# Conditioning rows and sums pinned, and the first stage of a two-layer backbone in a written-out order

## The chip, the cores and the metric

The kernel runs on one core of one Trainium2 chip. The metric is the device time of one execution in microseconds. Beside the plain runs one execution was taken by the hardware profiler; every row quoted here is from it. Engines are named as in the profile: PE is TensorE, DVE is VectorE, ACT is ScalarE, POOL is GpSimd, SP is the engine that issues most transfers. PEclk is the granted clock of TensorE as a share of full speed; it has two levels, 1.2 and 2.4 GHz.

## What is computed

A bidirectional hybrid backbone of two layers over 128 context tokens and 512 latent tokens, 1024 wide. What matters here, from the reference:

```
mod = silu(cond) @ ada_w + ada_b              # cond: c_ctx for context tokens, c for latent tokens
sh_m, sc_m, g_m, sh_f, sc_f, g_f = mod in six parts of 1024
h = rmsnorm(x, norm_mix) * (1 + sc_m) + sh_m
x = x + g_m * (token_mixers(h) @ w_out)       # mixers: one projection h @ w_in, HGRN2 and retention heads
h = rmsnorm(x, norm_ffn) * (1 + sc_f) + sh_f
x = x + g_f * ((silu(gate) * up) @ w_down)    # gate, up = h @ w_up
```

Outputs are the tokens after a final norm and the final states of the context tokens.

## The kernel before, in words

The 640 tokens are five tiles of 128 (tile 0 holds the context tokens). All weights come from memory as float32 through one stream (`Stream`, lines 56 to 100): `load` issues a transfer of 512 KB on SP, `cut` splits it into a rounded part on ACT (line 75) and the rest on DVE (line 76), and each GEMM is three matmuls per block (high by high, high by low, low by high). `W_BUFS` is 4, `RAW_BUFS` 3.

The modulation is computed in three ways. The four blocks that layer 0's first norm needs (block 0 and 2: scale, columns 0 to 511 and 512 to 1023; block 1 and 3: shift) are matmuls in `ada_first` (lines 322 to 491): each block is loaded in four quarters; blocks 0, 1 and 3 (`FAST`) are cut like weights (`cut`, lines 344 and 345) and multiplied (`mm`, line 355), block 2 is multiplied uncut in single precision (line 358); the row is copied out (line 363), turned into columns by eight small matmuls (`rt`, line 369) and finished on DVE (`fin`). The scales and shifts of the later norms are column sums on DVE (`ada_cols`, line 536): a tile of the transposed weights times a row of silu(c), which stands in all partitions (`srow`, loaded and activated in `ada_rows`, lines 514 and 515); 32 sums for layer 0's second norm and 64 for layer 1's two. The gates are accumulated on DVE (`ada_chunk`, line 505).

The first stage runs under `manual_schedule`: what `ada_first` and the first GEMM trace keeps its order on every engine. It does, per token tile t: `sq(t)` squares and sums on ACT, POOL's power makes the norm's factor, `xs(t)` scales on DVE, `tr(t)` transposes on PE, `xc(t)` copies to SBUF on ACT; then, per half of the 1024 columns, `full(t, hf)` applies scale and shift (`kd` of four 128-blocks on DVE, the others on ACT), and `split(t, hf)` cuts the result into the GEMM's operand `hT`. The GEMM (`ws`, line 610) has three units u (zf, zb and qa of head 0), each in two token parts hf (tokens 0 to 255 and 256 to 639) and two halves of K, so twelve pieces. In before the pieces of the first half of K are issued as soon as the blocks 0 and 1 are done, with the matmuls of blocks 2 and 3 between them:

```
out = [(0, 0, 0, 4), lambda: mm(2, 2, 4), (1, 0, 0, 4), lambda: rt(2), lambda: fin(2), ...
```

Everything else is put in order by a scheduler, which may issue an instruction early on its engine, the manual stage included, when its inputs and its buffer are there. The program order comes from a planner (`Net.run`, line 138): each piece of GEMM yields a cost in planner units, and side tasks in lanes advance a step whenever their quantum has been reached (`Q_ADA` 3.0 units in the mixer, 2.0 in the output projection, 4.0 in the feed-forward part; the lane starts 25 units late, `ACC0`). A unit of three 128-column GEMMs and so on costs what its `yield` says: 5.1e-3 per token and K half in `ws`, 1.31 per four blocks in `as_`. In the mixer `ORDER` (line 38) sets the order of heads; its units after the first three GEMM units add up to 216. `pin` (line 303) keeps an instruction behind the one traced before it on its engine.

Of the kernel before, what the change touches and what calls it, by code (L numbers as in the profile page):

```python
# [46 lines left out]
Q_SCAN = 2.65  # L47
Q_ADA = (3.0, 2.0, 4.0)
ADP_BUFS = 2


def view(t, off, dims):
# [3 lines left out]
class Stream:  # L56
# [5 lines left out]
    def load(self):  # L62
        src, kk, nn = self.slots[self.loaded]
        raw = self.net.rawp.tile([P, 1024], F32, tag="raw", name="raw")
        self.net.nc.sync.dma_start(out=raw[:, :kk * nn].rearrange("p (k n) -> p k n", k=kk), in_=src)
        self.raw[self.loaded] = (raw, kk, nn)
        self.loaded += 1

# [34 lines left out]
class Net:  # L103
# [218 lines left out]
    def ada_first(self):  # L322
        nc, a = self.nc, self.a
        V = nc.vector
        raws, xn, rs, xt = [], {}, {}, {}

        def load(i):
            col = (1 - i % 2) * 1024 + (i // 2) * 512
            for j in range(4):
                w = self.B("adw")  # L330
                nc.sync.dma_start(out=w[:, :1024].rearrange("p (k n) -> p k n", k=2),
                                  in_=a["ada_w"][0, 2 * j * P:(2 * j + 2) * P, col:col + 512].rearrange(
                                      "(k p) n -> p k n", p=P))
                raws.append(w)
        pr, pc, row, cuts = {}, {}, {}, {}

        def cut(i, j):
            w = raws[4 * i + j]
            if i < 2 or j == 2:
                hi, lo = self.whp.tile([P, 1024], F32R, tag="wh", name="ahi"), \  # L340
                    self.wlp.tile([P, 1024], F32R, tag="wl", name="alo")
            else:
                hi, lo = self.ON("ahi", F32R)[:, :1024], self.ON("alo", F32R)[:, :1024]
            nc.scalar.copy(hi, w[:, :1024])
            V.tensor_tensor(lo, w[:, :1024], hi.bitcast(F32), op=ALU.subtract)
            cuts[i, j] = hi, lo

        def mm(i, j0, j1):
            if j0 == 0:
                pr[i] = self.ps("pr")  # L350
            for k in range(2 * j0, 2 * j1):
                sl = slice(k % 2 * 512, k % 2 * 512 + 512)
                if i in FAST:
                    for n, wv in enumerate(cuts[i, k // 2]):
                        nc.tensor.matmul(pr[i][:, :512], self.srv[:, k], wv[:, sl],
                                         start=k == 0 and n == 0, stop=k == KT - 1 and n == 1)
                else:
                    nc.tensor.matmul(pr[i][:2, :512], self.sT[:, :, k], raws[4 * i + k // 2][:, sl],
                                     start=k == 0, stop=k == KT - 1)
            if j1 == 4:  # L360
# [29 lines left out]
        def tr(t):  # L390
            xt[t] = self.norm_b(t, xn[t])
# [22 lines left out]
            nc.scalar.copy(hi, f)  # L414
            V.tensor_tensor(lo, f, hi.bitcast(F32), op=ALU.subtract)

        load(0)
        for t in range(NT):
            self.load_x(t)
        load(1)  # L420
        for _ in range(3):
            self.W.load()
        load(2)
        self.new_hT()
        for j in range(4):
            cut(0, j)
            if j == 3:
                sq(0)
            mm(0, j, j + 1)
        xs(0)  # L430
        sq(1)
        tr(0)
        xs(1)
        sq(2)
        xc(0)
        tr(1)
        xs(2)
        sq(3)
        xc(1)
        tr(2)  # L440
        xs(3)
        sq(4)
        xc(2)
        tr(3)
        self.setup_cols()
        rt(0)
        fin(0)
        cut(1, 0)
        mm(1, 0, 1)
        xs(4)  # L450
        xc(3)
        cut(1, 1)
        tr(4)
        mm(1, 1, 2)
        cut(1, 2)
        xc(4)
        cut(1, 3)
        mm(1, 2, 3)
        self.W.cut()
        mm(1, 3, 4)  # L460
        self.W.cut()
        load(3)
        nc.sync.dma_start(out=self.mask, in_=a["mask"].rearrange("p (b s) -> p b s", b=5))
        nc.sync.dma_start(out=self.rope, in_=a["rope"].rearrange("p (b s) -> p b s", b=2))
        rt(1)
        fin(1)
        mm(2, 0, 2)
        full(0, 0)
        full(1, 0, 4)
        split(0, 0)  # L470
        split(1, 0)
        for t in range(2, NT):
            full(t, 0)
            if t > 2:
                split(t - 1, 0)
        self.W.cut()
        split(4, 0)
        lb = self.setup_lb()
        cut(3, 0)
        cut(3, 1)  # L480
        out = [(0, 0, 0, 4), lambda: mm(2, 2, 4), (1, 0, 0, 4), lambda: rt(2), lambda: fin(2),
               lambda: cut(3, 2), (0, 1, 0, 4), lambda: mm(3, 0, 2), lambda: cut(3, 3), lb, (1, 1, 0, 4),
               lambda: mm(3, 2, 4), lambda: rt(3), lambda: fin(3), (2, 0, 0, 4), (2, 1, 0, 4)]
        for t in range(NT):
            out.append(lambda t=t: full(t, 1, 4 if t == 1 else KD))
            if t:
                out.append(lambda t=t: split(t - 1, 1))
        out.append(lambda: split(NT - 1, 1))
        out += [(u, hf, 4, 8) for hf in range(2) for u in range(3)]
        out.append(self.W.pump)  # L490
        return out

    def ada_chunk(self, l, col, alloc, sink):
# [15 lines left out]
    def ada_rows(self):  # L509
        a = self.a  # L510
        self.srow = self.const.tile([P, 2, DM], F32, name="srow")
        self.junk = self.const.tile([P, DM], F32, name="junk")
        for c, src in enumerate((a["c_ctx"], a["c"])):
            self.nc.sync.dma_start(out=self.srow[:, c], in_=bass.AP(src.tensor, src.offset, [[0, P], [1, DM]]))
        self.nc.scalar.activation(self.srow, self.srow, AF.Silu)

    def ada_cols(self, l, m, alloc):
        V = self.nc.vector
        if self.srow is None:
            self.ada_rows()  # L520
# [89 lines left out]
    def ws(self, *evacs, mid=None, order=None):  # L610
# [4 lines left out]
        mm = self.nc.tensor.matmul  # L615
        base = self.W.used

        def part(u, hf, k0, k1):
            hi, lo = slots[u]
            sl = slice(cut, TOK) if hf else slice(0, cut)  # L620
            o = pss[u][:, 512 - cut + sl.start:512 - cut + sl.stop]
            for k in range(k0, k1):
                h_hi, h_lo = self.hT[:, 0, k, sl], self.hT[:, 1, k, sl]
                mm(o, hi[:, k], h_hi, start=k == 0, stop=False)  # L624
                mm(o, hi[:, k], h_lo, start=False, stop=False)  # L625
                mm(o, lo[:, k], h_hi, start=False, stop=k == KT - 1)  # L626
        def both(u, k0, k1):
            hi, lo = slots[u]
            sls = [slice(0, cut), slice(cut, TOK)]
# [18 lines left out]
        for i, op in enumerate(order):  # L648
            if callable(op):
                op()  # L650
                continue
            u, hf, k0, k1 = op
            while mid and hf and self.pend:
                self.flush1()
            if pss[u] is None:
                pss[u] = self.ps("gw")
                slots[u] = self.W.get(base + u)
            part(u, hf, k0, k1)
            if mid and i == 1:
# [622 lines left out]
```

## Time and profile before

| | |
|---|---|
| plain runs, median of 3 | 1849.0 us (1847.05 to 1849.16) |
| the profiled execution | 1847.48 us |
| its span, first to last instruction | 1845.7 us |
| mean granted clock of PE | 0.991 |
| PE busy | 1793.7 us (97%) |
| DVE busy | 1041.3 us (56%) |
| ACT busy | 712.1 us (39%) |
| POOL busy | 49.1 us (3%) |
| moved by transfers | 184.06 MB, mean 100 GB/s |

The page's slices show PE busy at 90% or more in all of the 40 but the first (0.5) and the last (0.8). The busy time of a pipelined matmul overlaps that of the next, and its end is modelled, so a full PE is not PE at its peak: the interval from one matmul's start to the next is what counts. An idle time in brackets in a timeline is the engine's time without work ahead of that instruction, with what ended it. A timeline merges neighbours of one line ("x8"); their time runs from the first start to the last end.

### The profile page before, as it was taken

The numbers are of one execution on the slowest core, as the hardware profiler recorded it, in microseconds if no ns is written. First come the engines' busy times: TensorE is split into PE (matmuls) and PEld (weight loads), VectorE is DVE, ScalarE is ACT, GpSimd is POOL, SyncE is SP. The second block draws the span as 40 slices with busy tenths as digits, with TensorE's granted clock in tenths as the row PEclk, the third lists the DMA queues.
The fourth block names the chain that finished last, engine by engine and source line by source line (L and its number), as shares of the span: only waits on it lengthen the run. The fifth ranks groups of instructions, "written<-read, shape, count | busy, mean of one in ns | idle before, by whom it ended". The sixth has DMA issues, their size and how long they took to land.

```text
span 1845.7 us, 29294 instructions
## 1 busy us (share of the span) xinstructions
PE 1793.7 (97%) x12301; PEld 1719.7 (93%) x12301; DVE 1041.3 (56%) x1614; ACT 712.1 (39%) x1208; POOL 49.1 (3%) x59
## 2 busy tenths in 40 slices
PE   5999999999999999999999999999999999999998
PEld 3799999998999978999899999999899998899988
DVE  3889757864854986222366656587475522323234
ACT  5675645633522211222246555455352221122221
POOL 1000000000000000000000000000000000000000
PEclk7999999999999999999999999999999999999999
DMA  8424223222433654222222121322234322222221
GB/s 288 155 81 152 78 78 112 92 69 69 137 115 117 224 182 140 80 70 75 75 81 72 50 69 53 109 78 89 80 92 126 115 75 75 80 80 69 75 75 58
DMA packets 204612, 184.06 MB, mean 100 GB/s; under 512 B 6736, under 2 KB 172336, under 8 KB 204480
## 3 DMA queue, kind: packets, MB, share of 16 engines
q1 hardware_dynamic: 199584, 179.67, 30.8%
q10 hardware_dynamic: 4640, 2.43, 0.4%
q8 instruction: 96, 1.57, 0.4%
q0 software_dynamic: 256, 0.09, 0.1%
q14 instruction: 36, 0.29, 0.1%
HBM read 177.44 MB, written 4.72 MB: 99 GB/s over the span
## 4 chain that ended last, share of the span: by engine, by line
PE 78%; DVE 10%; DMA 4%; ACT 4%; issue 3%; SPq 1%; POOL 1%; DVEq 0%; POOLq 0%; ACTq 0%
PE gw L634 36%; PE ga L680 5%; PE ga L679 5%; PE ga L678 5%; PE ga L1053 5%; PE ga L1055 4%; PE ga L1054 4%; PE pl L771 3%; DMA adt<-in_ada_t 2%; DVE junk L536 2%; DVE wl L76 2%; PE gw L625 1%; PE gw L624 1%; PE gw L626 1%; PE ga L1032 1%
## 5 line engine op out<-in xcount | busy, mean ns | idle before, releaser
L634 PE MATMUL gw<-hT,wh 128*128 128x320 f32 x3712 | 702.0, 311 | 0.0
L634 PEld LDWEIGHTS gw<-hT,wh 128*128 128x128 f32 x3712 | 581.3, 188 | 1.1
L75 ACT CAST wh<-raw 128x1024 fp32r<-128x1024 f32 (+2 forms) x224 | 231.7, 1035 | 704.4 <-PE gw L634 267.1
L76 DVE TENSOR_TENSOR wl<-raw,wh 128x1024 fp32r<-128x1024 f32 (+2 forms) x224 | 269.4, 1204 | 357.3 <-ACT wh L75 357.1
L634 PE MATMUL gw<-hT,wl 128*128 128x320 f32 x1856 | 423.8, 309 | 0.0
L634 PEld LDWEIGHTS gw<-hT,wl 128*128 128x128 f32 x1856 | 310.4, 188 | 0.1
L678 PE MATMUL ga<-wh,hT 128*128 128x256 f32 x640 | 185.7, 290 | 0.0
L680 PE MATMUL ga<-wh,hT 128*128 128x256 f32 x640 | 181.4, 284 | 0.0
L679 PE MATMUL ga<-wl,hT 128*128 128x256 f32 x640 | 181.4, 283 | 0.0
L1053 PE MATMUL ga<-wh,act 128*128 128x512 f32 x330 | 130.2, 395 | 4.1 <-DVE xa L996 4.1
L1054 PE MATMUL ga<-wl,act 128*128 128x512 f32 x330 | 129.6, 393 | 0.0
L1055 PE MATMUL ga<-wh,act 128*128 128x512 f32 x330 | 128.8, 393 | 0.0
L536 DVE CUSTOM_DVE_ANT_0 junk<-adt,srow 128x1024 f32<-128x1024 f32 x96 | 117.8, 1227 | 18.5 <-DMA adt<-in_ada_t 17.0
L1104 DVE TENSOR_TENSOR sgf<-sgf,gw 128x640 f32<-128x640 f32 x44 | 36.1, 820 | 162.3 <-PE gw L634 162.3
L678 PEld LDWEIGHTS ga<-wh,hT 128*128 128x128 f32 x640 | 122.7, 192 | 0.3
L679 PEld LDWEIGHTS ga<-wl,hT 128*128 128x128 f32 x640 | 122.6, 192 | 0.3
L680 PEld LDWEIGHTS ga<-wh,hT 128*128 128x128 f32 x640 | 122.4, 191 | 0.0
L505 DVE SCALAR_TENSOR_TENSOR acc<-adw,sTt,acc 128x512 f32<-128x512 f32 x112 | 79.6, 747 | 23.0 <-DMA adw<-in_ada_w 22.7
L1053 PEld LDWEIGHTS ga<-wh,act 128*128 128x128 f32 x330 | 62.6, 190 | 18.6 <-DVE xa L996 6.0
L1055 PEld LDWEIGHTS ga<-wh,act 128*128 128x128 f32 x330 | 62.7, 190 | 13.3
L771 PE MATMUL pl<-X 128*128 128x128 f32 x560 | 72.3, 276 | 2.4 <-ACT X L758 2.3
L1054 PEld LDWEIGHTS ga<-wl,act 128*128 128x128 f32 x330 | 62.6, 190 | 12.5
(226 smaller groups left out, 2639.0 us busy)
## 6 DMA issues: line engine op xcount, KB each, us to landing
raw<-in_w_up SPq DMA_DIRECT2D x88, 512.0 KB, 3.8
raw<-in_w_in SPq DMA_DIRECT2D x72, 512.0 KB, 3.7
adt<-in_ada_t SPq DMA_DIRECT2D x48, 512.0 KB, 4.0
raw<-in_w_down SPq DMA_DIRECT2D x38, 512.0 KB, 3.7
adw<-in_ada_w SPq DMA_DIRECT2D x64, 256.0 KB, 2.9
adw<-in_ada_w SPq DMA_DIRECT2D x16, 512.0 KB, 7.0
raw<-in_w_out SPq DMA_DIRECT2D x16, 512.0 KB, 3.5
gate<-in_ada_b SPq DMA_DIRECT2D x8, 512.0 KB, 5.2
```

The source lines that it names most:

```text
L75: nc.scalar.copy(hi[:, :n], raw[:, :n])
L76: nc.vector.tensor_tensor(lo[:, :n], raw[:, :n], hi[:, :n].bitcast(F32), op=ALU.subtract)
L505: nc.vector.scalar_tensor_tensor(d, w, s, d, op0=ALU.mult, op1=ALU.add)
L536: V.tensor_tensor_reduce(out=self.junk, in0=w[:, :DM], in1=self.srow[:, c], scale=1.0, scalar=0.0, op0=ALU.mult, op1=ALU.add, accum_out=se ...
L634: mm(o, w[:, k], self.hT[:, d, k, sl], start=k == 0 and i == 0, stop=k == KT - 1 and i == 2)
L678: mm(o, a_hi, hi[:, j], start=i == 0, stop=False)
L679: mm(o, a_hi, lo[:, j], start=False, stop=False)
L680: mm(o, a_lo, hi[:, j], start=False, stop=i == nk - 1)
L771: nc.tensor.matmul(pl[:, i * P:(i + 1) * P], X[:, TOK + i * P:TOK + (i + 1) * P], X[:, i * P:(i + 1) * P], start=True, stop=True)
L1053: mm(o, a_hi, hi[:, j], start=i == 0, stop=False)
L1054: mm(o, a_hi, lo[:, j], start=False, stop=False)
L1055: mm(o, a_lo, hi[:, j], start=False, stop=i == nk - 1)
```

## The change

- `srow`'s two transfers are issued behind the stream's last weight load so far, and the Silu comes four steps of the lane later and is pinned. Of the two column sums of each tile the first is pinned.
- The first stage is given by two lists: `BOOT_LOADS`, the order of the transfers (`Lij` is quarter j of block i, `xt` a token tile, `W` a weight), and `BOOT`, the order of the steps. `feed` issues loads as far as a limit on quarters held allows. All quarters' cuts use the weight buffers.
- The GEMM's pieces (`g` u hf K-half) all stand behind the last block's matmuls, in the order 010 110 210 001 101 200 100 201 011 000 111 211; a unit is evacuated when its four pieces are done, in whatever order (`seen`).
- The lower bounds (`setup_lb`) go ahead of `split31` and of `g011`; the mask and rotary tables are loaded behind all of `BOOT_LOADS`.

```diff
+BOOT_LOADS = (
+    "L00 x4 L01 L10 L02 L11 L12 L13 L03 L20 x2 x3 x0 x1 L21 L30 L22 L31 L32 L33 L23 W W W "
+).split()
+BOOT = (
+    "cut00 sq4 xs4 tr4 cut01 mm00 cut10 cols xc4 cut02 cut11 mm01 cut12 mm10 cut13 mm02 mm11 mm12 cut03 "
+    "mm13 sq2 xs2 mm03 sq3 mm20 rt1 xs3 tr2 fin1 sq0 sq1 rt0 xs0 tr3 fin0 mm21 xc2 full20-4 xs1 tr0 xc3 "
+    "cut30 full30-0 full40-4 cut31 tr1 cut32 cut33 mm30 split40 split30 mm22 mm31 xc0 W mm32 mm33 mm23 "
+    "rt3 fin3 rt2 split20 fin2 W g010 g110 xc1 full01-3 W g210 full11-4 full00-0 split01 split11 g001 "
+    "full21-4 full10-0 split10 split00 full31-4 split21 g101 g200 full41-0 g100 g201 split31 split41 g011 "
+    "g000 g111 g211 "
+).split()
...
         def cut(i, j):
-            w = raws[4 * i + j]
-            if i < 2 or j == 2:
-                hi, lo = self.whp.tile([P, 1024], F32R, tag="wh", name="ahi"), \
-                    self.wlp.tile([P, 1024], F32R, tag="wl", name="alo")
-            else:
-                hi, lo = self.ON("ahi", F32R)[:, :1024], self.ON("alo", F32R)[:, :1024]
+            w = raws.pop((i, j))
+            hi, lo = self.whp.tile([P, 1024], F32R, tag="wh", name="ahi"), \
+                self.wlp.tile([P, 1024], F32R, tag="wl", name="alo")
...
+        def feed(last=False):
+            while loads and (last or loads[0][0] != "L" or len(raws) < B_BUFS - 1 - min(NT, len(xt) + 2)):
+                o = loads.pop(0)
+                if o[0] == "L":
+                    load(int(o[1]), int(o[2]))
+                elif o[0] == "x":
+                    self.load_x(int(o[1]))
+                else:
+                    self.W.load()
...
+        out = []
+        for o in BOOT:
+            if o[0] == "g":
+                out.append((int(o[1]), int(o[2]), 4 * int(o[3]), 4 * int(o[3]) + 4))
+            elif out:
+                out.append(lambda o=o: step(o))
+            else:
+                step(o)
+        feed(True)
         nc.sync.dma_start(out=self.mask, in_=a["mask"].rearrange("p (b s) -> p b s", b=5))
         nc.sync.dma_start(out=self.rope, in_=a["rope"].rearrange("p (b s) -> p b s", b=2))
...
         out.append(self.W.pump)
+        lbs = []
+        out.insert(-7, lambda: lbs.append(self.setup_lb()))
+        out.insert(-5, lambda: lbs[0]())
         return out
...
         for c, src in enumerate((a["c_ctx"], a["c"])):
-            self.nc.sync.dma_start(out=self.srow[:, c], in_=bass.AP(src.tensor, src.offset, [[0, P], [1, DM]]))
-        self.nc.scalar.activation(self.srow, self.srow, AF.Silu)
+            with self.tc.issue_after(self.W.last.ins):
+                self.nc.sync.dma_start(out=self.srow[:, c], in_=bass.AP(src.tensor, src.offset, [[0, P], [1, DM]]))
...
         if self.srow is None:
             self.ada_rows()
-            yield
+            for _ in range(4):
+                yield
+            self.pin(self.nc.scalar.activation(self.srow, self.srow, AF.Silu))
...
             for c in range(2):
-                V.tensor_tensor_reduce(out=self.junk, in0=w[:, :DM], in1=self.srow[:, c], scale=1.0, scalar=0.0,
-                                       op0=ALU.mult, op1=ALU.add,
-                                       accum_out=self.modc[:, l, m, 1 - which, c, j:j + 1])
+                r = V.tensor_tensor_reduce(out=self.junk, in0=w[:, :DM], in1=self.srow[:, c], scale=1.0, scalar=0.0,
+                                           op0=ALU.mult, op1=ALU.add,
+                                           accum_out=self.modc[:, l, m, 1 - which, c, j:j + 1])
+                if c == 0:
+                    self.pin(r)
...
-            if hf == 1 and k1 == KT:
+            if seen.get((u, 0)) == KT and seen.get((u, 1)) == KT:
                 self.W.done()
                 evacs[u](pss[u][:, 512 - cut:512 - cut + TOK].rearrange("p (a b) -> p a b", a=2))
```

## Rows read from the trace of the kernel before

**Rows 1.** Table by stretches: length, PE, PEld, DVE, ACT, POOL, PEclk, DMA share, GB/s.

```profile
0.00:51.70 51.70, 29.49 (x99) 19.18 (x99) 22.25 (x43) 29.54 (x43) 8.26 (x20) 0.77 0.77 260
51.70:85.40 33.70, 31.63 (x185) 26.82 (x185) 27.38 (x60) 18.21 (x29) 4.03 (x2) 1.00 0.53 182
85.40:1845.70 1760.30, 1732.62 (x12019) 1673.67 (x12018) 991.70 (x1513) 664.33 (x1139) 36.84 (x37) 1.00 0.30 93
```

**Rows 2.** Timeline, first stage, ScalarE: start us, us, engine, line, operation [idle before].

```profile
5.58 1.04 ACT L344 CAST ahi<-adw 128x1024 fp32r<-128x1024 f32 x1 [2.61 <-DMA adw<-in_ada_w]
...
36.97 1.91 ACT L515 ACTIVATE srow<-srow 128x2048 f32<-128x2048 f32 x1 [10.47 <-DMA srow<-in_c]
```

**Rows 3.** Timeline, SP's queue, first stage.

```profile
26.91 0.74 SPq L514 DMA_DIRECT2D srow<-in_c_ctx  x1
```

**Rows 4.** Table by stretches, layer 0 feed-forward part, 670 to 700 us.

```profile
670.00:680.00 10.00, 5.90 (x26) 4.58 (x26) 8.45 (x18) 1.06 (x1) 0.00 (x0) 0.92 0.56 184
680.00:690.00 10.00, 10.00 (x34) 8.02 (x35) 7.52 (x13) 1.61 (x2) 0.00 (x0) 0.74 0.34 105
690.00:700.00 10.00, 10.00 (x46) 8.29 (x45) 8.58 (x14) 1.56 (x2) 0.00 (x0) 1.00 0.75 223
```

**Rows 5.** Waits from 580 to 730 us: total us, times, longest us.

```profile
DVE junk L536 <- DMA adt<-in_ada_t: 15.9, 12, 4.6
...
PE ga L1053 <- DVE xa L996: 4.1, 1, 4.1
```

**Rows 6.** Table by stretches, layer 0's mixer.

```profile
85.40:420.00 334.60, 326.73 (x2570) 323.64 (x2570) 253.68 (x434) 189.57 (x346) 14.88 (x9) 1.00 0.30 94
...
100.00:200.00 100.00, 96.67 (x739) 95.72 (x738) 84.80 (x170) 67.36 (x119) 6.60 (x3) 1.00 0.34 109
```

**Rows 7.** Table by stretches of line 536 alone (first column DVE).

```profile
100.00:200.00 100.00, 22.44 (x36) 1.00 0.34 109
```

**Rows 8.** Groups of instructions, 5 to 52 us: busy us, mean ns | idle.

```profile
L345 DVE TENSOR_TENSOR alo<-adw,ahi 128x1024 fp32r<-128x1024 f32 x8 | 9.7, 1223 | 15.5 <-ACT ahi L344 15.4
...
L344 ACT CAST ahi<-adw 128x1024 fp32r<-128x1024 f32 x8 | 8.3, 1052 | 4.0 <-DMA adw<-in_ada_w 4.0
...
L363 ACT COPY row<-pr 4x512 f32<-4x512 f32 x2 | 1.1, 566 | 2.1 <-PE pr L355 2.1
```

**Rows 9.** Timeline, TensorE, first stage: small matmuls and transposes.

```profile
21.71 1.06 PE L586 MATMUL pt<-ident,xn 128*128 128x128 f32 x8 [1.23 <-DVE xn L388]
...
26.71 1.91 PE L586 MATMUL pt<-ident,xn 128*128 128x128 f32 x8
...
46.14 5.64 PE L358 MATMUL pr<-adw,sTt 128*2 128x512 f32 x8
...
53.34 3.59 PE L358 MATMUL pr<-adw,sTt 128*2 128x512 f32 x8
...
58.49 1.05 PE L369 MATMUL pc<-sel,row 2*128 2x2 f32 x8
...
65.65 0.39 PE L355 MATMUL pr<-ahi,sr 128*128 128x512 f32 x1
...
67.26 0.40 PE L355 MATMUL pr<-alo,sr 128*128 128x512 f32 x1
```

**Rows 10.** Table by stretches, two stretches of the first stage.

```profile
16.00:20.00 4.00, 4.00 (x22) 3.95 (x23) 1.64 (x4) 2.99 (x6) 1.10 (x2) 0.57 1.04 392
...
33.00:40.00 7.00, 0.00 (x0) 0.00 (x0) 0.00 (x0) 3.03 (x3) 0.00 (x0) 0.52 0.75 290
```

**Rows 11.** Timeline, TensorE, GEMM of the first stage.

```profile
74.87 0.39 PE L625 MATMUL gw<-hT,wh 128*128 128x256 f32 x1 [1.28 <-DVE hT L415]
75.10 0.28 PE L626 MATMUL gw<-hT,wl 128*128 128x256 f32 x1
...
79.17 0.34 PE L624 MATMUL gw<-hT,wh 128*128 128x384 f32 x1
...
85.41 0.28 PE L678 MATMUL ga<-wh,hT 128*128 128x256 f32 x1
```

More of the change, by code (lines that the diff above doesn't have):

```diff
@@ L64, in load @@
         raw = self.net.rawp.tile([P, 1024], F32, tag="raw", name="raw")
-        self.net.nc.sync.dma_start(out=raw[:, :kk * nn].rearrange("p (k n) -> p k n", k=kk), in_=src)
+        self.last = self.net.nc.sync.dma_start(out=raw[:, :kk * nn].rearrange("p (k n) -> p k n", k=kk), in_=src)
         self.raw[self.loaded] = (raw, kk, nn)
@@ L324, in ada_first, with load @@
         V = nc.vector
-        raws, xn, rs, xt = [], {}, {}, {}
-        def load(i):
+        raws, xn, rs, xt = {}, {}, {}, {}
+        def load(i, j):
             col = (1 - i % 2) * 1024 + (i // 2) * 512
[L329 to L334, printed above, removed]
+            raws[i, j] = w = self.B("adw")
+            nc.sync.dma_start(out=w[:, :1024].rearrange("p (k n) -> p k n", k=2),
+                              in_=a["ada_w"][0, 2 * j * P:(2 * j + 2) * P, col:col + 512].rearrange(
+                                  "(k p) n -> p k n", p=P))
         pr, pc, row, cuts = {}, {}, {}, {}
         def cut(i, j):
-            w = raws[4 * i + j]
-            if i < 2 or j == 2:
-                hi, lo = self.whp.tile([P, 1024], F32R, tag="wh", name="ahi"), \
-                    self.wlp.tile([P, 1024], F32R, tag="wl", name="alo")
-            else:
-                hi, lo = self.ON("ahi", F32R)[:, :1024], self.ON("alo", F32R)[:, :1024]
+            w = raws.pop((i, j))
+            hi, lo = self.whp.tile([P, 1024], F32R, tag="wh", name="ahi"), \
+                self.wlp.tile([P, 1024], F32R, tag="wl", name="alo")
             nc.scalar.copy(hi, w[:, :1024])
@@ L346, in cut, with mm @@
             cuts[i, j] = hi, lo
-        def mm(i, j0, j1):
-            if j0 == 0:
+        def mm(i, j):
+            if j == 0:
                 pr[i] = self.ps("pr")
-            for k in range(2 * j0, 2 * j1):
+            for k in (2 * j, 2 * j + 1):
                 sl = slice(k % 2 * 512, k % 2 * 512 + 512)
                 if i in FAST:
-                    for n, wv in enumerate(cuts[i, k // 2]):
+                    for n, wv in enumerate(cuts[i, j]):
                         nc.tensor.matmul(pr[i][:, :512], self.srv[:, k], wv[:, sl],
@@ L357, in mm @@
                 else:
-                    nc.tensor.matmul(pr[i][:2, :512], self.sT[:, :, k], raws[4 * i + k // 2][:, sl],
+                    nc.tensor.matmul(pr[i][:2, :512], self.sT[:, :, k], raws[i, j][:, sl],
                                      start=k == 0, stop=k == KT - 1)
-            if j1 == 4:
+            raws.pop((i, j), None)
+            if j == 3:
                 nr = 4 if i in FAST else 2
@@ L415, in split @@
             V.tensor_tensor(lo, f, hi.bitcast(F32), op=ALU.subtract)
[L417 to L423, printed above, removed]
-        self.new_hT()
[L425 to L462, printed above, removed]
+        loads = list(BOOT_LOADS)
+        def feed(last=False):
[7 more added lines that the diff above has]
+                    self.W.load()
@@ new lines, in ada_first, with step @@
+        do = {"cut": cut, "mm": mm, "sq": sq, "xs": xs, "tr": tr, "xc": xc, "rt": rt, "fin": fin, "split": split,
+              "cols": self.setup_cols, "W": self.W.cut}
+        def step(o):
+            feed()
+            n = o.rstrip("0123456789-")
+            args, _, kd = o[len(n):].partition("-")
+            if n == "full":
+                full(*map(int, args), int(kd))
+            else:
+                do[n](*map(int, args))
+        self.new_hT()
+        out = []
[4 more added lines that the diff above has]
+                out.append(lambda o=o: step(o))
+            else:
+                step(o)
@@ L463, in ada_first @@
+        feed(True)
         nc.sync.dma_start(out=self.mask, in_=a["mask"].rearrange("p (b s) -> p b s", b=5))
         nc.sync.dma_start(out=self.rope, in_=a["rope"].rearrange("p (b s) -> p b s", b=2))
[L465 to L487, printed above, removed]
@@ L488, in ada_first @@
-        out.append(lambda: split(NT - 1, 1))
-        out += [(u, hf, 4, 8) for hf in range(2) for u in range(3)]
         out.append(self.W.pump)
+        lbs = []
+        out.insert(-7, lambda: lbs.append(self.setup_lb()))
+        out.insert(-5, lambda: lbs[0]())
         return out
@@ L616, in ws @@
         base = self.W.used
+        seen = {}
         def part(u, hf, k0, k1):
             hi, lo = slots[u]
+            new = not seen.get((u, hf))
+            seen[u, hf] = seen.get((u, hf), 0) + k1 - k0
+            end = seen[u, hf] == KT
             sl = slice(cut, TOK) if hf else slice(0, cut)
@@ L623, in part @@
                 h_hi, h_lo = self.hT[:, 0, k, sl], self.hT[:, 1, k, sl]
-                mm(o, hi[:, k], h_hi, start=k == 0, stop=False)
+                mm(o, hi[:, k], h_hi, start=new and k == k0, stop=False)
                 mm(o, hi[:, k], h_lo, start=False, stop=False)
-                mm(o, lo[:, k], h_hi, start=False, stop=k == KT - 1)
+                mm(o, lo[:, k], h_hi, start=False, stop=end and k == k1 - 1)
         def both(u, k0, k1):
```

## The prediction

> **What bounds the kernel now.** The page comes first: TensorE's slices are full from the second of the 40 on, so time can only come from the start, from TensorE's few waits and from stretches in which its clock is low. The table by stretches splits the span: up to 51.7 us TensorE is busy for 29.5 us, at a mean granted clock of 0.77; then come 33.7 us in which the first three GEMM units and the second half of the modulation share TensorE; the remaining 1760.3 us hold 1732.6 us of TensorE work, so at most 27.7 us of gaps [rows 1]. The first 85.4 us are the place to look, and everything behind them moves with them as one block.
>
> Inside them ScalarE's timeline shows the largest hole: ScalarE, whose queue is in order, sat 10.47 us in front of the Silu of the conditioning rows (line 515) until their transfer landed at 36.97 [rows 2]. That Silu belongs to a later task and was put into ScalarE's queue ahead of the last token tile's copy and of block 1's last cast. SP's timeline shows why the rows came so late: their transfers were issued from 26.9 on, behind the 20 loads ahead of them [rows 3]. The second place is far later: between 670 and 690 the clock falls, and matmuls are missing. In these 20 us 60 matmuls ran, where the ten us behind them hold 46 [rows 4]: 32 are missing, at 4.6 per us **7.0 us**. The chain of waits around it says why: TensorE waited 4.1 us for a DVE operation (line 996), and DVE itself stood for 15.9 us, in 12 places, in front of layer 1's column sums (line 536), for tiles not yet there [rows 5].
>
> **The change part by part.** *The rows pinned.* Their transfers go behind a weight load, the Silu keeps its place in the program. The 10.47 us of waiting and the 1.91 us of Silu leave the first stage. The Silu comes back in the mixer, where ScalarE is busy for 189.6 of 334.6 us [rows 6]: hidden; if ScalarE were late there, 1.9 us would be the cost. What was queued behind it (a copy, casts, weight cuts) is released; next late is the data itself.
>
> *The stage in the new order.* All four blocks' matmuls come ahead of the GEMM, which so starts after a longer preparation and runs unbroken. I work out when its first piece can start.
> Loads: 24 of half a megabyte (16 block quarters, 5 token tiles, 3 weights). In before the first was there at 5.58 (the first cast), the 22nd at 36.97 [rows 2]: 21 in 31.4 us, 1.49 us each. Block 3's last quarter is now the 20th: 5.6 + 19 x 1.49 = 33.9; block 2's last is there at 35.4, the weights at 36.9, 38.4 and 39.9. Cast 1.05 and subtraction 1.22 [rows 8] make 36.2; four matmuls at 0.23 make 37.1; block 2's last quarter, half of the 3.59 us that eight took, 38.9; the row's copy 0.57, 39.5; the eight small transposing matmuls 1.05, **40.5** [rows 8, 9]. This is the lower end.
> TensorE's own queue gives the other end, since it is in order and nothing of the GEMM may pass. Ahead of the first piece stand 48 matmuls of 128x512 (from 65.65 to 67.26 seven intervals, 0.23 each; twice that at the lower clock), 16 of the single-precision kind (0.45, at the lower clock 0.71), 40 transposes (0.13 or 0.24) and four rounds of small ones (1.05, doubled 2.1) [rows 9]: 11.0 + 7.2 + 5.3 + 4.2 = 27.7 us at the high level, 22.1 + 11.3 + 9.6 + 8.4 = 51.4 at the low one. They start at about 10 us (the first block is cut at 5.6 + 2.3 = 7.9, and a token tile's transposes stand ahead of it). So 38 without any wait, which the loads forbid, or 61. In the first 51.7 us the mean granted clock was 0.77: 27.7 / 0.77 = 36, with 10 makes 46. The new queue has fewer holes than the old one, where no matmul ran from 33 to 40 [rows 10], but it does wait for loads. I take **45**, nearest to the row of this very stage.
> In before the granted clock went to 0.57 from 16 to 20, after TensorE had nearly stood still, and to 0.52 from 33 to 40, when it stood [rows 10]; steady work brought it back. The Trainium skill (TensorE: Matmul & The Clock Gate, "HAM oscillation — how this bites in real kernels") has a rule against this order: bursts of matmuls shorter than the transfer waits between them bring the slow clock back at every wait. By that rule the first piece would start at 61 and not at 45.
> The other engines stay below that. ScalarE did 29.5 us of work up to 51.7 [rows 1]; four casts and two row copies more and the Silu less make 32.9, from 5.6 on 38.5 without waits; DVE's 22.3 and four subtractions make 27.1. POOL's powers lie beside them.
> GEMM: six pieces of 12 matmuls over 384 columns and six over 256. From 79.17 to 85.41 ran three of the first kind, 2.08 each; from 75.10 to 79.17 (34 matmuls) the second kind took 0.12 a matmul, 1.43 a piece [rows 11]. 6 x 2.08 + 6 x 1.43 = **21.1 us**. The fourth piece is the first of the second half of K and starts 6.2 us in; its two tiles are modulated and split behind that cover. In before the like wait was 1.28 us [rows 11]; I take none, and 1.3 us is the price without the cover. The lower bounds' power and its small DVE operations sit beside the last pieces, ahead of the gates that need them: hidden.
> So the stage ends at 45 + 21.1 = 66 where it ended at 85.4: **19.4 us less** (bounds 23.8, from 40.5, and 3.3, from 61).
> SP too: mask and rotary tables now follow the 24 loads, at about 36 instead of 50, and the next weights follow them, needed only at 66. Nothing.
>
> *The sums pinned.* 96 sums of 1.23 us keep the planner's places; layer 0's 32 now all run in the mixer, two every 6 units of the planner's clock. From the stage's end to the output projection its own costs add up to 216 units, which took 334.6 us, 1.55 each [rows 6]: 2.6 us of sums in 9.3, 28% of DVE. From 100 to 200 DVE was busy for 84.8 us, 22.4 of them sums [rows 6, 7]; 62 + 28 is 90%. It stays below full, but a matmul may now wait behind a pair of sums: between 0 and 4 us, TensorE waiting there for 3.3 now; I take **1.5 lost**. Queued on DVE behind a pinned sum are the weight splits and the recurrence's steps, and behind those TensorE.
> Layer 1's 64 sums the same pin spreads over the feed-forward part; the tiles land well before their sums, and no evacuation stands behind a sum that waits. Of the 7.0 us I count **6 gained** (bounds 0 and 7).
>
> *Sum.* The profiled execution took 1847.5 us (span 1845.7 and 1.8 around it), 1.5 below the median of 1849.0. 1847.5 - 19.4 - 6 + 1.5 = 1823.6; between its own time and the median I say **1824**.
>
> **The rivals.**
> *Only the stage gains* (0.20): the stall near 679 stays, or another evacuation waits behind a pinned pair. For it: those 15.9 us of waiting [rows 5], and the pin leaves the tiles' buffers as they are. Against it: the waits come from sums running faster than tiles arrive. 1847.5 - 19.4 + 1.5 = 1830.
> *DVE becomes the bound in the mixer* (0.07): it is at 85% from 100 to 200 [rows 6]; 7 us given back instead of 1.5, 1829.
> *The pins don't hold everything* (0.05): the column tiles' own transfers (line 527) are not pinned, and up to four could be put among the block loads on SP, 4 x 1.49 = 6 us later: 1830.
> *TensorE at 1.2 GHz up to the GEMM* (0.10): start at 61, end at 82: 1847.5 - 3.3 - 6 + 1.5 = 1840. This is what the skill's rule above would bring.
> *The same, but through the GEMM as well* (0.03), the one that ends **slower**: the pieces take twice as long, 42 us, and the stage ends at 61 + 42 = 103, 18 later than now: 1847.5 + 18 - 6 + 1.5 = 1861. It decides from a stage end of about 94 on (85.4, the 4.5 gained elsewhere, and 3.7). For it: the half clock from 33 to 40 [rows 10]. Against it: before's pieces ran at 0.12 a matmul, the higher level, with other work ahead of them [rows 11].
>
> **How the numbers follow.** Forecast 0.55, rivals 0.20, 0.07, 0.05, 0.10, 0.03. A measurement of this kernel tells 0.2%, 3.7 us, from no change. Every case but the last is faster by more than that; of the clock rival's 0.10 I put 0.02 within 0.2%, for a clock that lingers into the GEMM. Faster 0.95, same 0.02, slower 0.03. Range: low end with the start at 40.5 (23.8), 7 for the stall and the mixer's 3.3 us of waits gone: 1813; high end at the clock rival, 1840.
>
> **What would show it.** Right: ScalarE has no wait before line 515 in the first 60 us; the first GEMM matmul at 41 to 47; twelve pieces without a break in 21 us, the last matmul near 66; no line 536 ahead of that; sums spread over 100 to 250 and over the feed-forward part past 800; no gap at the first change of output columns, where line 1053 waited. Wrong: a first piece later than 50 with the granted clock at 0.5 before it; loads landing slower than 1.49 us; a wait of TensorE for DVE that before does not have; a stage that ends at 66 and a span that shrinks by less than 15.

## The result, and the profile after

The changed kernel takes **1821.8 us** (median of four runs, 1820.74 to 1822.84), the kernel before beside it on the same chip 1848.0 (1846.88 to 1849.16): a ratio of 0.9858, 95% interval 0.9841 to 0.9875, faster by 26 us. Forecast was 1824, between 1813 and 1840. The profiled execution took 1822.63 us, with a span of 1820.9.

The table by stretches of the kernel after (length, PE, PEld, DVE, ACT, POOL, PEclk, DMA share, GB/s), cut where the first GEMM piece starts, where the stage ends and where the mixer ends, answers to [rows 1] and [rows 6]; the last row, 560 to 710 us, is the place of [rows 4]:

```profile
0.00:40.40 40.40, 30.59 (x139) 19.44 (x139) 24.92 (x44) 30.10 (x42) 8.88 (x21) 1.00 0.99 337
40.40:63.20 22.80, 22.80 (x145) 22.79 (x146) 15.35 (x43) 16.02 (x29) 3.29 (x1) 0.93 0.57 190
63.20:1820.90 1757.70, 1731.49 (x12020) 1671.98 (x12018) 1000.27 (x1527) 668.97 (x1142) 38.50 (x37) 1.00 0.31 95
63.20:402.30 339.10, 328.34 (x2573) 324.00 (x2571) 261.96 (x448) 194.09 (x349) 16.50 (x9) 1.00 0.32 98
...
560.00:710.00 150.00, 150.00 (x840) 136.37 (x839) 84.92 (x119) 30.19 (x34) 0.00 (x0) 1.00 0.43 132
```

To be seen: up to 40.4 TensorE is busy for 30.6 us where it was for 29.5 in 51.7, at a mean granted clock of 1.00 in place of 0.77 (though the matmuls up to about 14 us ran at the lower rate, as the timeline below shows); the GEMM then has no gap (22.80 of 22.80); the mixer is longer (339.1, it was 334.6); from 560 to 710 TensorE never stands. With marks at the same matmuls of both kernels (the first `ga` matmul at the stage's end; then, among the matmuls over 512 columns that write `ga`, line 1053 before and 1035 after, the first of layer 0's output projection, the first of its `w_down` and the last of that line), the span splits into these terms:

| | before | after | difference | predicted |
|---|---|---|---|---|
| stage end | 85.4 | 63.2 | −22.2 | −19.4 |
| mixer, to the output projection | 334.6 | 339.1 | +4.5 | +1.5 |
| on to layer 0's `w_down` | 221.0 | 221.0 | 0.0 | 0 |
| from there to the last `w_down`, with the stall | 1156.8 | 1150.0 | −6.8 | −6 |
| rest | 47.9 | 47.6 | −0.3 | 0 |
| span | 1845.7 | 1820.9 | −24.8 | −23.9 |

ScalarE's timeline of the kernel after (start us, us, engine, line, operation [idle before]) answers to [rows 2]:

```profile
30.86 2.97 ACT L350 CAST ahi<-adw 128x1024 fp32r<-128x1024 f32 x3
33.74 1.14 ACT L421 CAST hT<-xt 128x512 fp32r<-128x512 f32 x2
34.78 1.01 ACT L402 COPY xt<-pt 128x1024 f32<-128x1024 f32 x1
36.84 1.04 ACT L86 CAST wh<-raw 128x1024 fp32r<-128x1024 f32 x1 [1.05 <-PE pr L361]
...
99.49 1.28 ACT L495 ACT_TABLE_LOAD   x1
100.78 1.91 ACT L495 ACTIVATE srow<-srow 128x2048 f32<-128x2048 f32 x1
```

The wait of 10.47 us is gone, the Silu (now line 495) stands at 100.8, and it brought a table load of 1.28 us with it. TensorE's timeline of the same kernel answers to [rows 9, 11]:

```profile
9.98 1.97 PE L562 MATMUL pt<-ident,xn 128*128 128x128 f32 x8 [6.49 <-DVE xn L395]
11.60 0.77 PE L361 MATMUL pr<-ahi,sr 128*128 128x512 f32 x1
...
24.32 1.09 PE L562 MATMUL pt<-ident,xn 128*128 128x128 f32 x8
...
36.75 1.88 PE L364 MATMUL pr<-adw,sTt 128*2 128x512 f32 x4
38.56 1.94 PE L376 MATMUL pc<-sel,row 4*128 4x2 f32 x16
40.44 0.45 PE L605 MATMUL gw<-hT,wh 128*128 128x384 f32 x1
...
63.22 0.28 PE L660 MATMUL ga<-wh,hT 128*128 128x256 f32 x1
```

From its first transpose at 9.98 to the first piece at 40.44 TensorE's queue takes 30.5 us, and between 8 and 63 us the table of waits gives it one wait only, those 6.5 us at the start. Eight transposes took 1.97 us at 9.98 and 1.09 at 24.32: the queue began at the lower rate, which the table's 1.00 does not show.

### The profile page after: what moved, and what is told of

It is laid out like the page before. It is cut to its first block, busy times and chain, and to the rows that moved or that the text cites. A ratio compares the mean times of both kernels' runs of the same rounds, so it can differ in the third digit from the quotient of the medians.

```text
span 1820.9 us, 29285 instructions
## 1 busy us (share of the span) xinstructions
PE 1784.9 (98%) x12301; PEld 1714.2 (94%) x12301; DVE 1040.5 (57%) x1613; ACT 715.1 (39%) x1211; POOL 50.7 (3%) x59
## 4 chain that ended last, share of the span: by engine, by line
PE 83%; DVE 8%; ACT 4%; issue 2%; DMA 2%; POOL 1%; SPq 0%; POOLq 0%; DVEq 0%; ACTq 0%
PE gw L616 39%; PE ga L1035 5%; PE ga L1037 5%; PE ga L1036 5%; PE ga L662 5%; PE ga L661 5%; PE ga L660 5%; PE pl L753 3%; DMA adw<-in_ada_w 2%; DVE wl L87 1%; PE gw L606 1%; PE gw L607 1%; PE gw L605 1%; PE ga L1014 1%; PE ga L1013 1%
## 5 line engine op out<-in xcount | busy, mean ns | idle before, releaser
L86 ACT CAST wh<-raw 128x1024 fp32r<-128x1024 f32 (+2 forms) x224 | 231.7, 1035 | 706.7 <-PE gw L616 271.5
L753 PEld LDWEIGHTS pl<-X 128*128 128x128 f32 x560 | 67.8, 191 | 7.7 <-ACT X L740 7.1
```

Of the source, the lines that this page charges most:

```text
L86: nc.scalar.copy(hi[:, :n], raw[:, :n])
L753: nc.tensor.matmul(pl[:, i * P:(i + 1) * P], X[:, TOK + i * P:TOK + (i + 1) * P], X[:, i * P:(i + 1) * P], start=True, stop=True)
```

## The experiments

All are made from the changed kernel unless said otherwise. In the table of stretches below, all from one profiled execution of each, "stage end" and the others are the marks of the table above.

| run | first piece | stage end | mixer | first to last `w_down` | time |
|---|---|---|---|---|---|
| before | 51.7 | 85.4 | 334.6 | 1156.8 | 1847 to 1848 |
| after | 40.4 | 63.2 | 339.1 | 1150.0 | 1821.8 |
| 1 pins, old stage | 37.9 | 70.5 | 339.4 | 1150.0 | 1830.1 |
| 2 rows free | 50.2 | 74.1 | 341.7 | 1150.2 | 1835.4 |
| 3 sums free | 40.8 | 62.0 | 337.9 | 1157.6 | 1827.7 |
| 4 sums of layer 1 pinned only | 40.3 | 61.5 | 337.5 | 1149.8 | 1822.1 |
| 5 block 2, a quarter | 41.5 | 64.3 | 339.4 | 1149.4 | 1824.0 (one execution) |
| 6 block 2 cut | 56.4 | 80.1 | 339.1 | 1153.2 | 1841.6 |
| 7 short sums in layer 0 | 40.5 | 63.3 | 336.7 | 1150.0 | 1820.1 (one execution) |
| 8 one step ahead of the Silu | 40.6 | 61.8 | 341.6 | 1150.5 | 1824.2 |
| 9 no Silu | 40.5 | 63.3 | 339.2 | 1152.7 | 1825.5 (one execution) |
| 10 no Silu, short sums | 40.4 | 61.6 | 336.3 | 1150.9 | 1819.0 (one execution) |
| 11 ten steps ahead of the Silu | 40.6 | 61.8 | 337.7 | 1150.0 | 1821.7 |

**1. The pins in the old stage.** Made from the kernel before, with the rows' and sums' edits alone.

```diff
-            self.nc.sync.dma_start(out=self.srow[:, c], in_=...)
-        self.nc.scalar.activation(self.srow, self.srow, AF.Silu)
+            with self.tc.issue_after(self.W.last.ins):
+                self.nc.sync.dma_start(out=self.srow[:, c], in_=...)
...
+            for _ in range(4):
+                yield
+            self.pin(self.nc.scalar.activation(self.srow, self.srow, AF.Silu))
...
+                if c == 0:
+                    self.pin(r)
```

> The kernel before with the two pins alone (rows and sums); the first stage keeps its old order. Theory, the terms of the trace: the 10.5 us wait for the rows and the 1.9 us of Silu leave ScalarE's queue, so the first stage ends some 10 to 12 us earlier than at 85.4; the missing 6.7 us at 670 to 690 come back; the mixer gives back 4.5 us as in the changed kernel. Together 1848 - 11 - 6.7 + 4.5 = 1835, ratio 0.993. Rival, the pins are worth nothing without the new order because the blocks' loads and casts end the stage anyway: the stage still ends at 85, 1848 - 6.7 + 4.5 = 1846.

Measured: 1830.1 us, ratio 0.9907 (0.9893 to 0.9920). The stage ends at 70.5, 14.9 earlier, where 10 to 12 had been expected; the stall's 6.8 are gained; the mixer is 4.8 longer. So about two thirds of the gain are the pins' alone. The new order is worth the rest, 8.3 us in time. In this kernel the first piece starts at 37.9, earlier than with the new order, but the pieces share TensorE with blocks 2 and 3 for 32.6 us.

**2. The rows free, in the new order.**

```diff
-            with self.tc.issue_after(self.W.last.ins):
-                self.nc.sync.dma_start(...)
+            self.nc.sync.dma_start(...)
+        self.nc.scalar.activation(self.srow, self.srow, AF.Silu)
...
-            for _ in range(4):
-                yield
-            self.pin(self.nc.scalar.activation(self.srow, self.srow, AF.Silu))
+            yield
```

> The changed kernel with the rows' transfers and the Silu as in before (not pinned, one step of the lane), sums pinned, new order. Theory: the two transfers are put among the block loads on SP, two half-megabyte loads or 3 us later, and the Silu stands in ScalarE's queue in the first stage and waits for them: first piece 3 to 8 us later, at 44 to 48, total 1825 to 1830. Rival, the new order fills SP so that the transfers come behind its loads anyway: first piece at 40.4, total within 2 us of 1821.8.

Measured: 1835.4 us, 0.9935 (0.9922 to 0.9947), 13.7 us more than the change. The edit takes out two things, the pin and three of the lane's four steps; run 8 below takes out the three steps alone, costs 2.4 us and shows the same longer mixer (341.6 and 341.7). So the rows' pin itself is worth about 11 us in the new order. ScalarE's timeline of this kernel:

```profile
45.99 1.91 ACT L487 ACTIVATE srow<-srow 128x2048 f32<-128x2048 f32 x1 [7.18 <-DMA srow<-in_c]
47.81 0.56 ACT L370 COPY row<-pr 2x512 f32<-2x512 f32 x1
```

Its table of waits from 30 to 52 us, TensorE (total us, times, longest us):

```profile
PE pc L376 <- ACT row L370: 8.8, 2, 8.5
```

The Silu went into ScalarE's queue right ahead of the copy of block 2's row and waited 7.2 us for its transfer. The row's copy stood behind it, TensorE's small matmuls behind the copy, the whole GEMM behind those, and the first piece started 9.8 us later. TensorE's granted clock was 0.53 from 42 to 50 us, when it stood for most of the time, and 0.50 still from 50 to 54, and the pieces took 23.9 us in place of 22.8. It is the mechanism of [rows 2] in another place.

**3 and 4. The sums free, and pinned in layer 1 only.**

```diff
-                r = V.tensor_tensor_reduce(...)
-                if c == 0:
-                    self.pin(r)
+                V.tensor_tensor_reduce(...)
```

> The changed kernel without the pin of the column sums; rows pinned, new order. Theory: the mixer loses its 4.5 us again and the stall of 6.7 us near 650 comes back, unless free sums get into the first stage: 1821.8 - 4.5 + 6.7 = 1824, and the first GEMM piece still starts at 40.4. Rival, the free sums are put among the first stage's DVE work as in before (nine by 86 us) and hold the splits up: first piece or the pieces behind it late by 5 us or more, 1829.

```diff
-                if c == 0:
+                if c == 0 and l == 1:
```

> The changed kernel with the sums pinned in layer 1 only. Theory: the pin in layer 0 costs the mixer 4.5 us and the pin in layer 1 earns 6.7: without the former 1821.8 - 4.5 = 1817.3, mixer 334.6 us from the stage's end to the output projection, no stall near 650. Rival, the 4.5 us come from the stage ending earlier and not from the pin (less DVE work is done ahead of the mixer): mixer stays at 339 us, 1822.

Measured: 1827.7 us free, 0.9889 (0.9876 to 0.9903); 1822.1 with layer 1's alone, 0.9867 (0.9852 to 0.9882). The waits of the kernel with free sums, 560 to 740 us:

```profile
DVE junk L510 <- DMA adt<-in_ada_t: 17.0, 11, 4.7
...
PE ga L1033 <- DVE xa L976: 5.0, 1, 5.0
```

That is [rows 5] again, and the stretch from the first to the last `w_down` is back at 1157.6; with layer 1's sums pinned it is 1149.8. (One of the four executions with free sums took 1824.0, the others 1827.3 to 1828.7; the one profiled is of the longer ones.) So **the pin of layer 1's 64 sums is what removes the stall**, and nothing else in the change does. Layer 0's pin takes 1.2 to 1.6 us of mixer; that is less than what separates the runs of one kernel, and the time without it is the same. Run 4's theory had put all of the mixer's 4.5 us down to that pin; for the larger part they are not its.

**5 and 6. Block 2.** Its 16 single-precision matmuls are TensorE's slowest work in the stage. Run 5 leaves out twelve of them (three quarters of block 2's contraction, so scale columns 512 to 1023 are not the reference's); run 6 cuts block 2 like the others, which replaces them by 16 of the fast kind and adds four casts and four subtractions.

```diff
-                else:
+                elif j == 3:
...
-                                     start=k == 0, stop=k == KT - 1)
+                                     start=k == 6, stop=k == KT - 1)
```

> The changed kernel with three quarters of block 2's single-precision matmuls left out (12 of 16; the scale of columns 512 to 1023 is then wrong); its loads and everything else stay. Theory A, TensorE's own queue sets the start of the GEMM: 5.6 us of its work less, so the first piece comes earlier than 40.4, as far as the first weight's rest allows, which was ready at 39.15: 39.2 to 39.5, and TensorE shows idle time of about 4 us before it. Theory B, the loads set it, as the prediction's lower end has it: no quarter arrives earlier, first piece at 40.4 and TensorE idle before the last quarters.

```diff
-FAST = (0, 1, 3)
+FAST = (0, 1, 2, 3)
...
-    "mm13 sq2 xs2 mm03 sq3 mm20 ..."
+    "mm13 sq2 xs2 mm03 sq3 cut20 mm20 ..."
```

(`cut21`, `cut22` and `cut23` come in the same way, each right ahead of its matmuls.)

> The changed kernel with block 2 cut like the others (four casts on ScalarE, four subtractions on DVE more, and 16 single-precision matmuls of 0.47 replaced by 16 of 0.23 each). Theory A, TensorE's queue sets the start: 3.8 us less on it, first piece up to 1.2 us earlier at 39.2, total 1 us less, within 0.2% of the changed kernel. Rival, ScalarE and DVE have no room between 30 and 40 us: four more casts and subtractions, 4.2 and 4.9 us, put the last cut and the splits back by 3 to 5 us: first piece at 43 to 45, total 1825 to 1827.

Measured: the first piece of run 5 starts at 41.5, **later** than in the kernel after, though TensorE has 5.6 us less to do, and neither theory holds. The table by stretches, kernel after and then run 5:

```profile
22.00:26.00 4.00, 4.00 (x26) 2.61 (x24) 1.95 (x7) 3.78 (x8) 1.65 (x3) 1.00 1.03 393
26.00:30.00 4.00, 4.00 (x24) 2.27 (x24) 3.35 (x10) 3.35 (x5) 0.94 (x1) 1.00 1.05 387
```

```profile
22.00:26.00 4.00, 2.79 (x24) 2.56 (x24) 1.89 (x6) 3.84 (x10) 1.49 (x3) 0.98 1.03 392
26.00:30.00 4.00, 4.00 (x23) 3.93 (x24) 2.92 (x9) 2.01 (x4) 1.17 (x2) 0.59 1.05 388
```

With the matmuls gone TensorE had holes (2.79 of 4 us), and the granted clock fell to 0.59 behind them. The token tiles' transposes then ran slowly (24 in 4.46 us, where eight take 1.09 in the kernel after), ScalarE, which copies them out, reached block 3's first cast at 29.8 in place of 28.4, and DVE cut that block's last three quarters 1.4 us later. The kernel after, then run 5:

```profile
31.93 3.50 DVE L351 TENSOR_TENSOR alo<-adw,ahi 128x1024 fp32r<-128x1024 f32 x3 [0.24 <-ACT ahi L350]
```

```profile
33.37 3.50 DVE L351 TENSOR_TENSOR alo<-adw,ahi 128x1024 fp32r<-128x1024 f32 x3 [0.23 <-ACT ahi L350]
```

In the kernel after these cuts end at 35.4 and the matmuls that read the last of them start at 36.0, so TensorE's queue was ahead of DVE's cuts as the limit by half a microsecond only, and taking work out of it alone could gain little. Run 6, 1841.6 us, 0.9970 (0.9958 to 0.9981), is the extreme case. Its stretches and TensorE's waits, 8 to 56 us:

```profile
26.00:30.00 4.00, 4.00 (x17) 3.33 (x16) 0.51 (x5) 1.12 (x3) 0.73 (x2) 0.50 1.05 387
30.00:38.00 8.00, 8.00 (x34) 7.16 (x33) 5.24 (x12) 4.48 (x8) 0.64 (x1) 0.50 1.11 332
```

```profile
PE pr L361 <- ACT ahi L350: 7.7, 3, 3.1
```

Four more casts stand in ScalarE's queue right ahead of the matmuls that need them; TensorE waits for ScalarE, is at 1.2 GHz from 26 to 38 us, and ScalarE then waits for its transposes. The first piece starts at 56.4, 16 us late: 20 of the 26 us of gain are gone, without a transfer more (17 of them by the stage's end; 3.2 stand far behind, in the stretch to the last `w_down`). Most of it is thus waiting and low clock, since the edit itself makes TensorE's work shorter. Run 5 shows that the long single-precision matmuls cost nothing here while they fill TensorE's waiting. The two runs do not part what the low clock costs from what the place in ScalarE's queue costs; other places for the four casts were not tried.

**7 to 11. The mixer's 4.5 us.** Run 7 sums 64 of 1024 columns in layer 0 (its second norm's modulation lacks what is left out); run 8 puts one step of the lane ahead of the Silu, where the change has four, and run 11 ten; run 9 copies the rows without Silu (the same modulation from raw conditioning); run 10 is runs 7 and 9 together.

```diff
+                ns = DM if l else 64
-                r = V.tensor_tensor_reduce(out=self.junk, in0=w[:, :DM], in1=self.srow[:, c], ...
+                r = V.tensor_tensor_reduce(out=self.junk[:, :ns], in0=w[:, :ns], in1=self.srow[:, c, :ns], ...
```

> The changed kernel with layer 0's 32 column sums over 64 columns instead of 1024 (the scales and shifts of layer 0's second norm are then wrong): about 1.1 us less on DVE each, 36 us in all; steps, loads and pins stay. Theory, the sums' DVE time in the mixer is what it gives back: from the stage's end to the output projection 339.1 falls to 334 or below. Rival, the order does it (steps later in the lane, other instructions put ahead): the mixer stays within 1.5 us of 337.5 to 339.

```diff
-            for _ in range(4):
-                yield
+            yield
```

> The changed kernel with one step of the lane before the Silu instead of four; the pins stay. Theory, the sums then start nine planner units earlier, which the mixer's DVE can take: total within 0.2% of 1821.8. Rival, the three steps matter because the Silu, pinned, waits for its rows on ScalarE and holds the recurrence's copies up: a wait of ScalarE for the rows of several us, total 1825 or more.

```diff
-            self.pin(self.nc.scalar.activation(self.srow, self.srow, AF.Silu))
+            self.pin(self.nc.scalar.copy(self.srow, self.srow))
```

> The rows are copied instead of put through Silu, so layer 0's feed-forward modulation is computed from raw conditioning; ScalarE then loads no function table for them. In the changed kernel two table loads of 1.28 us more stand in the mixer (one ahead of the Silu at 99.5, one behind it at 104.7). Theory A (DVE's sums delay the evacuations, the tables are hidden): the mixer stays at 339.1, within 0.7, time about 1822. Theory B (the 2 us that the shortened sums did not give back are ScalarE's: the table loads delay the copies of X): mixer 337 or less, time about 1820.

(Run 10: the edits of runs 7 and 9.)

> The same, and layer 0's sums over 64 of 1024 columns as before. With both gone theory B says a mixer of 334.6 to 335, what it took in the kernel before, time about 1818; theory A says 336.7, as with the shortened sums alone, and the rest lies in other places of the planner's order.

```diff
-            for _ in range(4):
+            for _ in range(10):
```

> Ten steps instead of four ahead of the Silu, so the rows and layer 0's sums come some 20 us later. One step made the mixer 2.5 us longer than four did. If an early start is what costs, ten steps give 337 to 338.5 and a time of 1820 to 1821; if the sums cost wherever they stand, 339 and 1822; a second rival is that they fall into the stretches from 300 us on in which DVE is already at 18.8 of 20: 341 or more, 1824.

Measured: with short sums the mixer takes 336.7, 2.4 less. Without Silu it takes 339.2, as with it, and with both edits 336.3. Theory B's numbers did not come, but the run is a weak test of it: the mixer still has seven table loads, as many as with the Silu (the first two at 102.4 and 104.9, where they had been at 99.5 and 104.7). Better is TensorE's timeline of the kernel after around the Silu, from 97 to 111 us; its only wait is this one:

```profile
109.74 2.05 PE L786 MATMUL pu<-va,kT 128*128 128x128 f32 x16 [0.52 <-ACT kT L781]
```

So the Silu and its table loads cost TensorE 0.5 us of waiting at most there. One step ahead of the Silu makes the mixer 341.6, ten make it 337.7. The later start is the cheaper one, but not all of the 2.5 us between one step and four is the sums' own. The same part of the mixer, in the kernel after and then in run 8, whose sums begin in it:

```profile
83.20:103.20 20.00, 18.59 (x136) 18.18 (x135) 17.34 (x51) 13.11 (x20) 1.05 (x1) 1.00 0.30 87
```

```profile
81.80:101.80 20.00, 16.72 (x110) 16.27 (x109) 18.71 (x46) 13.42 (x21) 1.03 (x1) 0.91 0.37 113
```

TensorE waited 3.3 us there for a copy of the recurrence, where it waits 1.4 in the kernel after, and behind that wait its granted clock was 0.50 (93.7 to 97.1). Its busy time in the mixer is 1.7 us longer for the same matmuls, its idle time 0.8 us. Run 2, with the same one step, shows the same 3.3 us and the same drop behind it.

Run 8 took 1824.2 us, 0.9876 (0.9861 to 0.9891); run 11 1821.7, 0.9863 (0.9847 to 0.9880), no better than the change by a measurement. Run 9's time is above its forecast for a reason outside the mixer: its last stretch is 2.7 us longer. Layer 1's mixer shows the same pattern there: TensorE waited 1.8 us for DVE at 1190, where it waits 1.0 in the kernel after, and its granted clock was then 0.50 from 1192.3 to 1195.7. Run 6's 3.2 us have a like pair, a wait of 2.5 us and 0.50 from 1208.8 to 1212.2. Why those waits were longer stays open.

Where the sums act is plain in DVE's and ScalarE's timelines of the kernel after:

```profile
141.61 0.83 DVE L757 TENSOR_TENSOR QQ<-QQ,F 128x640 f32<-128x640 f32 x1
142.34 1.23 DVE L510 CUSTOM_DVE_ANT_0 junk<-adt,srow 128x1024 f32<-128x1024 f32 x1
143.49 0.09 DVE L510 DVE_READ_ACCUMULATOR2_ANT modc<- 128x1 f32 x1
143.49 0.83 DVE L758 TENSOR_TENSOR KK<-KK,F 128x640 f32<-128x640 f32 x1
```

```profile
144.35 0.72 ACT L740 COPY X<-KK 128x640 f32<-128x640 f32 x1 [1.16 <-DVE KK L758]
```

A sum of 1.2 us stands between two steps of the recurrence. ScalarE's copy waits 1.16 us for the second step, and TensorE's next matmul (line 753) waits 1.7 us for the copy, at 145.1. In the 20 us ahead of it DVE was full:

```profile
120.00:140.00 20.00, 20.00 (x165) 20.00 (x164) 20.00 (x34) 13.00 (x23) 1.54 (x1) 1.00 0.32 96
```

TensorE's waits for such copies in the whole mixer (total us, times, longest us), in the kernel before, in the kernel after and in run 7:

```profile
PE pl L771 <- ACT X L758: 2.3, 3, 1.3
```

```profile
PE pl L753 <- ACT X L740: 5.1, 5, 1.7
```

```profile
PE pl L755 <- ACT X L742: 2.5, 3, 1.4
```

With short sums these waits are back near what they were, and the 2.6 us are the mixer's 2.4. One wait of 1.3 to 1.4 us, at 90.5 in the kernel after, is in all three; it stands ahead of the first sum there and is not the sums'. Run 4, with full sums that are free in layer 0, has 2.5 as well, and 1.4 us of a wait for the state in their place: what a sum costs is a matter of where it falls. What stays open is the other 1.7 to 2.1 us: runs 7 and 10 still take 336.7 and 336.3, not 334.6. The kernel before had 7.9 us of TensorE idle in the mixer and the kernel after 10.8, which is 2.9 of the 4.5; the other 1.6 us the profile books as busy time, in nearly the same instructions.

## Why the prediction was right

- **Sum.** 1823.6 was worked out for the profiled execution, which took 1822.6. Three terms were each off, and two of the errors cancel: the stage gained 2.8 more, the mixer gave back 3.0 more, the stall gained 0.8 more. That the sum came within 1 us is therefore luck in part; the terms are right to about 3.
- **Rows pinned, the Silu hidden: right.** The first stage no longer waits for it. What I left out are table loads: ScalarE has seven in the mixer, where before has five. Around the Silu they cost TensorE half a microsecond of waiting at most (experiments 7 to 11). The Trainium skill (ScalarE activation tables: per-element evaluation and per-set limits, "What a function is on this engine") prices one at 1283 ns, and the rows show 1.28.
- **Start of the first piece: the term was mis-sized.** I took 45, between 40.5 by the loads and 61 by a slow TensorE; it started at 40.44. The step that failed is the division of TensorE's 27.7 us by the clock of the old stage, 0.77. The new queue had no holes, the granted clock was 1.00 for most of it, and 30.5 us went by from 9.98 on: my 27.7 for the higher level and some 3 more, about 2 of them from the first 4.5 us, which ran at the lower rate. That this equals the lower end by the loads is chance: the loads came sooner than I had them (block 3's three last casts ran back to back from 30.9 to 33.8, where I had the last quarter landing at 33.9), and what ended last was TensorE's own queue, with DVE's cuts half a microsecond ahead of it.
- **GEMM 21.1 us: right where the clock held.** In five of the nine profiled kernels with this order the twelve pieces took 21.2; in the one profiled here 22.8, for the reason of the last section.
- **TensorE at 1.2 GHz up to the GEMM: did not come for the change.** The table of waits has none of TensorE for a transfer, and the granted clock was 1.00 from 16 to 20 and from 33 to 40, where it had been 0.57 and 0.52 [rows 10]. By the rule of the Trainium skill that the prediction quotes (TensorE: Matmul & The Clock Gate, "HAM oscillation — how this bites in real kernels"), of bursts shorter than transfer waits, the start would have been at 61. But runs 5 and 6 show how near it was: holes from waits for ScalarE and DVE, rather than for transfers, brought 0.5, and run 6 came out at 1841.6, next to the 1840 of the clock rival.
- **Mixer: the term was mis-sized, 4.5 against 1.5, and just outside its bounds of 0 to 4.** The mechanism is the one named, a matmul behind a pair of sums, for 2.4 to 2.8 of it (runs 7 and 10); the rest has no cause shown. The bound was drawn from TensorE's own 3.3 us of waits; DVE's mean of 90% hid that single stretches reach 20.00 of 20.
- **Stall: right.** 6.8 of the 7.0 that the missing matmuls gave, and runs 3 and 4 tie it to the pin of layer 1's sums. The rival "only the stage gains" falls.
- **What would show it:** no wait ahead of the Silu, twelve pieces without a break, the first sum (line 510) at 102.7 and the last at 857.5, no gap at the change of output columns: all came as written, but for the pieces' time, 22.8 us instead of 21. The first piece fell just below the stated 41 to 47, and the stage's end at 63.2 instead of 66.

## What to carry to other kernels

An instruction whose input comes late does its harm in the in-order queue it is put into: look for the longest wait of an engine that is not the bound, and ask what stands behind it; here one Silu cost about 11 us, and some 55 us later almost nothing. Do not price a reordered stage at the old stage's mean clock: ask what waits the new queue will have, and beware of taking filler out of it, since the work that bridges a wait may be what keeps the clock. When a run is a microsecond or two off, look for a stretch at the lower clock behind a wait before blaming the instructions themselves. Work that is moved "beside" a chain on another engine costs where it falls between two links of that chain, so look at the fullest short stretch of that engine, not at its mean.

## What the hardware showed that I had not expected

TensorE's clock dropped in a stretch in which it had no idle time by the profile, and not in every execution. Stretch 42 to 45 us of the kernel after, and then of run 4, which issues the same there:

```profile
42.00:45.00 3.00, 3.00 (x11) 3.00 (x11) 2.84 (x9) 3.00 (x7) 0.00 (x0) 0.50 1.06 384
```

```profile
42.00:45.00 3.00, 3.00 (x19) 3.00 (x18) 2.85 (x8) 2.87 (x6) 0.00 (x0) 1.00 1.07 377
```

Eleven matmuls in place of nineteen, and a GEMM of 22.8 us in place of 21.2. Of nine profiled kernels with this order of the stage, four (after, runs 5, 7 and 9) show 0.50 to 0.65 there and five show 1.00. Just ahead, from 36.75 to 40.44, TensorE ran four single-precision matmuls with two columns of weights and sixteen matmuls of two columns. That these bring the drop was not tested. Its 1.6 us are of the size of the 2.1 us by which the four runs of the changed kernel differ, and the two longer ones (1822.6 and 1822.8) show a mean clock of 0.998, the two shorter ones (1820.7 and 1820.9) 0.999.
